# Pairs in the first feed-forward block, the norm's factor moved behind the products, and VectorE's pair work rearranged

## The chip, the cores and the metric

The kernel runs on one core of a Trainium2 chip. Its time is the device time of one execution in microseconds (us); before the change it is 1032.45 us, the median of 3 runs (1032.17 to 1032.88).

## What is computed

One trunk layer on x of shape (1, 256, 2048) in float32. A projection of the normed input feeds four differential-attention heads and a conformer convolution; their outputs, side by side, go through an output projection and are added to x, which gives h. Then comes the part that the change touches, a gated feed-forward block with 5632 hidden columns:

```
h  = h + mixed @ w_out
hn = rms_norm(h, norm2_g)              # h * rstd2 (per row) * g2 (per column)
a  = hn @ w_gate ;  bu = hn @ w_up     # 2048 -> 5632
y  = h + (silu(a) * bu) @ w_down
```

## The kernel before

**Precision by splitting.** Every operand of a matmul is split into a rounded part `hi` (float32r) and the remainder `lo`, and a product is three matmuls: hi*hi, lo*hi, hi*lo. ScalarE makes `whi` of the weights (L326), VectorE subtracts to get `wlo` (L335). For some units a second way makes `wlo`: ScalarE writes the negated weights (L329) and a DMA on GpSimd's queue adds the weights to it (L330); these are the units that `BY_DMA` names.

**Units.** The work is a list `chunks`, one entry per unit. A plain unit is two k-tiles (128 rows each) of one weight matrix times 512 columns: 2 x 2 x 3 = 12 matmuls of 128x512. `run_chunks` goes through the list with a hand-written order: at step t it splits units up to t + 2 and rounds units up to t + 2, or t + 3 when a pair is near (`lead`, `HI_AHEAD`, `LO_AHEAD`), then multiplies unit t. In the middle and at the end of a unit it calls `resume()`, which takes every running side generator one `yield` further; that is how sums, transposes and forms are put between units.

**Blocks.** The feed-forward part has 11 blocks j of 512 hidden columns, each with 16 gate and 16 up k-tiles, in three groups of 4, 4 and 3; after each group come two passes of the down projection. Blocks 1 to 10 and the down passes use a scheme of the Strassen kind: a *pair* takes k-tiles p and p + 8 of both matrices and makes 7 products (`PRODUCTS`, 21 matmuls) in place of 8 (24 matmuls). The other 8 k-tiles (`REST`, taken in twos) stay plain units, "g" for gate and "u" for up; "s" is a pair. `ORDER = "sggsggsuusuu"`, and block 1 has `FIRST_ORDER`. The products go to eight PSUM banks, `acc` for the first four and `aux` for the others; `bank_sums` (L1182) adds them on VectorE, `products_done` applies silu and `block_done` multiplies.

A pair costs VectorE and ScalarE this (`b` are the four loaded tiles, `t` four sums of them): three subtractions and additions (L1049 to L1051, `round_pair`), a cast of `b` on ScalarE (L1052), then in `split_pair` a cast of the sums (L1055) and the remainders `wlb` and `wlt` (L1058, L1059). `wt`, which holds `t`, has one buffer; `wb`, `wh`, `wlb` and `wlt` have two.

**Block 0** is plain: 8 gate units and 8 up units with `fh`, the split operands of h. The forms of h that pairs need, with the norm's factor `rstd2` multiplied in, are made beside it by `make_forms` (L984 to L1032): it spreads the factor over the columns by two transposes (L988), multiplies the rows by it (L996), and makes sums and splits. `out_done` runs after each of the four column groups n of the output projection: it adds to h (L828), transposes h (L846), scales by g2 (L851), splits (L853, L854), and copies h out to DRAM on GpSimd's queue (L823).

**Memory.** A pool `pre` holds everything up to the feed-forward part, h included; after the last column group it is closed and a pool `ffn` takes its place.

Of the kernel before, what the change touches and what calls it, by code (L numbers as in the profile page):

```python
# [18 lines left out]
P = 128  # L19
# [14 lines left out]
LINE = 128  # L34
EPS = 1e-6
# [51 lines left out]
FIRST_ORDER = "gsggsgsuusuu"  # L87
# [16 lines left out]
PAIR_BUFS = 2  # L104

# [24 lines left out]
def tile_block(  # L130
# [13 lines left out]
    prestack = ExitStack()  # L144
    pre = prestack.enter_context(tc.tile_pool(name="pre", bufs=2))
    small = prestack.enter_context(tc.tile_pool(name="small", bufs=4))
# [4 lines left out]
    h = [pre.tile([P, D], F32, tag=f"h{m}", name=f"h{m}", bufs=1) for m in range(NM)]  # L151
# [255 lines left out]
    def run_chunks():  # L407
# [4 lines left out]
        loaded, split = set(), set()  # L412
# [8 lines left out]
        def split_next():  # L421
            chunks[j]["split"](chunks[j])
            split.add(j)

# [3 lines left out]
        def freed(side, t):  # L428

            which, bufs = ((raws, RAW_BUFS), (pairs, PAIR_BUFS))[side]  # L430
            if not ahead[side] or pairs[2] - 1 not in loaded:
                return None
            k = which[place[side][ahead[side][0]] - bufs]
            return k if k in split and (t >= k or not chunks[k]["by_dma"]) else None

# [7 lines left out]
        for t in range(n):  # L443
# [33 lines left out]
    def square_sum(src, accum, **kw):  # L477
        junk = pre.tile([P, N], F32, tag="junk", name="junk", bufs=1)
# [107 lines left out]
    def conv_back(b):  # L586
# [37 lines left out]
        for b in range(2):  # L624
            for t in range(NB // 2):
# [6 lines left out]
                for j in range(2):  # L632
# [3 lines left out]
                    hi = pre.tile([P, S], F32R, tag="mchi", name=f"mchi{ct}", bufs=NCT)  # L636
                    lo = pre.tile([P, S], F32R, tag="mclo", name=f"mclo{ct}", bufs=NCT)
# [135 lines left out]
    def attend_values(hd):  # L773
# [29 lines left out]
        for e in range(2):  # L803
            mixa[2 * hd + e] = lhs_pair("a", 2 * hd + e) if hd >= 2 else tuple(
                pre.tile([P, S], F32R, tag=t, name=t, bufs=4) for t in ("mahi", "malo"))
# [7 lines left out]
    hT = {}  # L813

    hn = []
# [9 lines left out]
    def out_done(n, ps):  # L825
        cs = slice(n * N, (n + 1) * N)
# [13 lines left out]
        for t in range(0, N // P, 2):  # L840
# [6 lines left out]
            if k % HK == 0:  # L847
                hn.append(early.tile([P, HK, S], F32, tag="wb", name="hn"))
            rows = hn[k // HK][:, k % HK : k % HK + 2, :]
            for i in range(2):  # L850
                act.activation(rows[:, i, :], pt[:, i, :], AF.Copy, scale=col("g2", k + i))  # L851
            hi, lo = lhs_two("h", k)
            act.copy(hi, rows)  # L853
            dve.tensor_tensor(lo, rows, hi.bitcast(F32), ALU.subtract)  # L854
            for i in range(2):
                hT[k + i] = (hi[:, i, :], lo[:, i, :])
# [3 lines left out]
        else:  # L860
            yield
            yield
            prestack.close()
            ffn["pool"] = ctx.enter_context(tc.tile_pool(name="ffn", bufs=1))
            start(make_forms())


    ffn = {}
    actT = {}
    sil = {}  # L870

    def silu_done(ps):
        yield
        for m in range(NM):
            sil[m] = ffn["pool"].tile([P, N], F32, tag=f"sum{m}", name="sil")
            act.activation(sil[m], ps[m], AF.Silu, scale=rstd2[m])

    def up_done(j, ps):
        fp = ffn["pool"]
        aa = []  # L880
        for m in range(NM):
            a = fp.tile([P, N], F32, tag=f"sum{2 + m}", name="a")
            dve.scalar_tensor_tensor(a, ps[m], rstd2[m], sil[m], ALU.mult, ALU.mult)
            aa.append(a)
        yield from lag(4)
        yield from transposed(j, aa)

    def transposed(j, aa):
        last = j + 1 in FIRSTS and NDS[group_of(j)[0]] < HD
        b = j - group_of(j)[1]  # L890
        for t in range(N // P // 2):
# [9 lines left out]
            if b < 2 and 2 * t < nd:  # L901
                if not b and not t:
                    raw_act[g] = ffn["pool"].tile([P, 2, nd, S], F32, tag="draw", name="raw_act")
# [30 lines left out]
    def make_down_forms(g):  # L934
# [20 lines left out]
        hs = ffn["pool"].tile([P, 2, nd, P], F32R, tag="dhs", name="dhs")  # L955
# [12 lines left out]
        ls = ffn["pool"].tile([P, 4, nd, P], F32R, tag="draw", name="dls")  # L968
# [11 lines left out]
    def make_forms():  # L980
        fp = ffn["pool"]
        rep = fp.tile([P, S], F32, tag="sum1", name="rep")
        for m in range(NM):
            act.activation(rep[:, m * P : (m + 1) * P], ident, AF.Identity, bias=rstd2[m], scale=0.0)  # L984
        yield
        ps = aux_ps.tile([P, N], F32, tag="aux", name="ps_r")
        for m in range(NM):
            pe.transpose(ps[:, m * P : (m + 1) * P], rep[:, m * P : (m + 1) * P], ident)  # L988
        yield
        rb = fp.tile([P, S], F32, tag="sum2", name="rb")  # L990
        act.copy(rb, ps[:, :S])
        yield
        for i in range(2):
            for k in range(0, HK, 4):
                t = hn[i][:, k : k + 4, :]
                dve.tensor_tensor(t, t, rb.unsqueeze(1).to_broadcast([P, 4, S]), ALU.mult)  # L996
                yield

        nr = HK - NS
        chi = fp.tile([P, 2 * nr, S], F32R, tag="chi", name="chi")  # L1000
        clo = fp.tile([P, 2 * nr, S], F32R, tag="clo", name="clo")
        for i in range(2):
            act.copy(chi[:, i * nr : (i + 1) * nr], hn[i][:, NS:])
        yield
        for i in range(2):
# [370 lines left out]
```

## Time and profile before

| what | value |
|---|---|
| time, median of 3 | 1032.45 us |
| span of the profiled execution | 1030.8 us |
| TensorE (PE) busy | 1025.7 us, 100% |
| VectorE (DVE) busy | 929.2 us, 90% |
| ScalarE (ACT) busy | 643.4 us, 62% |
| GpSimd (POOL) busy | 102.7 us, 10% |
| block 0 begins / block 1 begins | 338.3 / 383.1 us |

Of the profiled execution the span from its first to its last instruction is known, and it lies 1.65 us under the median of the timed runs. In rows of the timeline the first number is the start in us, the second the duration, then engine, line, operation, output <- inputs, shape and count; brackets give the idle time before it and what ended it. Rows of the table by stage give, for each engine, busy us and in brackets the number of instructions.

### The profile page before, as it was taken

How to read it: one execution, taken by the hardware profiler on the slowest of the kernel's cores; microseconds unless marked ns; L12 is line 12 of the kernel's file. 1: busy time of each engine (PE TensorE's matmuls, PEld its weight loads, DVE VectorE, ACT ScalarE, POOL GpSimd, SP SyncE). 2: the span in 40 equal slices, each digit the busy share in tenths (PEclk: the TensorE clock that was granted, in tenths of full speed). 3: DMA queues.
4: the chain of work that ended last, by engine and by line, in shares of the span. 5: the costliest groups of instructions: out<-in, count | busy, mean ns of one | idle time of the engine just before them, and what ended most of it. 6: DMA issues, size and time to landing. Idle time of an engine off the chain costs nothing.

```text
span 1030.8 us, 13034 instructions
## 1 busy us (share of the span) xinstructions
PE 1025.7 (100%) x4642; PEld 849.4 (82%) x4642; DVE 929.2 (90%) x1128; ACT 643.4 (62%) x786; POOL 102.7 (10%) x146
## 2 busy tenths in 40 slices
PE   9999999999999999999999999999999999999998
PEld 8888888888888888888888888888888888888887
DVE  6899999999765699999999898989999989889998
ACT  7644656665756675676666556667757556657562
POOL 0300112111000000100102101101001111010020
PEclk9999999999999999999999999999999999999999
DMA  9757555544466677997989799889798979897776
GB/s 338 254 194 258 190 184 164 158 169 166 141 215 214 197 262 222 282 265 210 254 259 272 251 257 270 258 234 262 228 269 255 285 207 283 247 267 218 226 200 174
DMA packets 116448, 238.64 MB, mean 232 GB/s; under 512 B 7840, under 2 KB 9120, under 8 KB 116384
## 3 DMA queue, kind: packets, MB, share of 16 engines
q1 hardware_dynamic: 105216, 203.58, 59.3%
q0 software_dynamic: 10880, 34.08, 17.0%
q8 instruction: 36, 0.59, 0.2%
q14 instruction: 28, 0.23, 0.1%
q10 hardware_dynamic: 288, 0.16, 0.1%
HBM read 204.24 MB, written 9.44 MB: 207 GB/s over the span
## 4 chain that ended last, share of the span: by engine, by line
PE 100%; POOL 0%; DVE 0%; issue 0%; POOLq 0%
PE acc L365 11%; PE acc L366 11%; PE acc L371 11%; PE q L1097 11%; PE q L1103 11%; PE q L1098 11%; PE q L1078 9%; PE q L1077 9%; PE q L1076 9%; PE ps_a L898 1%; PE ps_s L712 1%; PE ps_o L782 1%; PE ps_warm L164 0%; PE ps_h L846 0%; PE ps_qk L693 0%; PE ps_at L802 0%
## 5 line engine op out<-in xcount | busy, mean ns | idle before, releaser
L326 ACT CAST whi<-raw 128x1024 fp32r<-128x1024 f32 (+1 forms) x256 | 264.2, 1043 | 143.8 <-PE acc L366 86.6
L335 DVE TENSOR_TENSOR wlo<-raw,whi 128x1024 fp32r<-128x1024 f32 (+1 forms) x208 | 250.4, 1214 | 38.2 <-ACT whi L326 38.0
L1055 ACT CAST wh<-wt 128x2048 fp32r<-128x2048 f32 x61 | 116.8, 1915 | 109.9 <-DVE wt L1051 109.7
L1059 DVE TENSOR_TENSOR wlt<-wt,wh 128x2048 fp32r<-128x2048 f32 x61 | 139.8, 2291 | 19.8 <-ACT wh L1055 19.7
L1097 PE MATMUL q<-whi,chi 128*128 128x512 f32 x320 | 125.2, 391 | 0.0
L1098 PE MATMUL q<-whi,clo 128*128 128x512 f32 x320 | 124.6, 389 | 0.0
L365 PE MATMUL acc<-whi,xhi 128*128 128x512 f32 x312 | 124.1, 398 | 0.0
L366 PE MATMUL acc<-whi,xlo 128*128 128x512 f32 x312 | 122.2, 392 | 0.0
L1076 PE MATMUL q<-wh,fhi 128*128 128x512 f32 x280 | 109.8, 392 | 0.0
L1077 PE MATMUL q<-wh,flo 128*128 128x512 f32 x280 | 109.0, 389 | 0.0
L1058 DVE TENSOR_TENSOR wlb<-wb,wh 128x1536 fp32r<-128x1536 f32 x61 | 106.8, 1751 | 1.0 <-ACT wh L1052 1.0
L572 DVE SCALAR_TENSOR_TENSOR y<-upad,cw,y 128x256 f32<-128x256 f32 x240 | 101.6, 490 | 0.0
L330 POOL DMA_DIRECT2D wlo<-raw x48 | 41.5, 865 | 555.7 <-ACT wlo L329 286.3
L1052 ACT CAST wh<-wb 128x1536 fp32r<-128x1536 f32 x61 | 89.8, 1472 | 1.0 <-DMA wb<-in_w_down_dram 1.0
L1103 PE MATMUL q<-wlo,chi 128*128 128x512 f32 x320 | 85.7, 390 | 0.0
L371 PE MATMUL acc<-wlo,xhi 128*128 128x512 f32 x312 | 85.2, 394 | 0.0
L1049 DVE TENSOR_TENSOR wt<-wb 128x1024 f32<-128x1024 f32 x61 | 74.4, 1220 | 0.0
L1097 PE MATMUL q<-whi,ahi 128*128 128x512 f32 x182 | 71.0, 390 | 0.0
L1098 PE MATMUL q<-whi,alo 128*128 128x512 f32 x182 | 70.9, 389 | 0.0
L1103 PEld LDWEIGHTS q<-wlo,chi 128*128 128x128 f32 x320 | 60.0, 188 | 12.7 <-DMA wlo<-raw 0.3
L1097 PEld LDWEIGHTS q<-whi,chi 128*128 128x128 f32 x320 | 60.1, 188 | 12.3
L1098 PEld LDWEIGHTS q<-whi,clo 128*128 128x128 f32 x320 | 60.1, 188 | 12.2
(260 smaller groups left out, 1850.5 us busy)
## 6 DMA issues: line engine op xcount, KB each, us to landing
raw<-in_w_in_dram SPq DMA_DIRECT2D x78, 512.0 KB, 4.6
raw<-in_w_gate_dram SPq DMA_DIRECT2D x48, 512.0 KB, 5.0
raw<-in_w_up_dram SPq DMA_DIRECT2D x48, 512.0 KB, 5.3
wlo<-raw POOLq DMA_DIRECT2D x48, 512.0 KB, 7.1
raw<-in_w_down_dram SPq DMA_DIRECT2D x46, 512.0 KB, 6.2
wb<-in_w_down_dram SPq DMA_DIRECT2D x42, 512.0 KB, 5.9
wb<-in_w_up_dram SPq DMA_DIRECT2D x40, 512.0 KB, 4.4
wb<-in_w_gate_dram SPq DMA_DIRECT2D x40, 512.0 KB, 5.5
```

The source lines that it names most:

```text
L326: act.copy(c["hi"], c["raw"])
L335: dve.tensor_tensor(c["lo"], c["raw"], c["hi"].bitcast(F32), ALU.subtract)
L365: pe.matmul(ps[m], xhi[:, ms], hi[:, j, :], start=c["first"] and j == 0, stop=False)
L366: pe.matmul(ps[m], xlo[:, ms], hi[:, j, :], start=False, stop=False)
L371: pe.matmul(ps[m], xhi[:, ms], lo[:, j, :], start=False, stop=c["last"] and j == nk - 1)
L1055: act.copy(c["hi"][:, :SUMMED], c["t"])
L1059: dve.tensor_tensor(lot, c["t"], c["hi"][:, :SUMMED].bitcast(F32), ALU.subtract)
L1076: pe.matmul(ps, hi, c["hi"][:, w], start=bool(first), stop=False)
L1077: pe.matmul(ps, lo, c["hi"][:, w], start=False, stop=False)
L1097: pe.matmul(ps, xs[i][0][:, ms], hi[:, i, :], start=i == 0 and bool(c["first"].get(qs[m])), stop=False)
L1098: pe.matmul(ps, xs[i][1][:, ms], hi[:, i, :], start=False, stop=False)
L1103: pe.matmul(sum_bank(c, qs[m]), xs[i][0][:, ms], lo[:, i, :], start=False, stop=i == 1 and bool(c["last"].get(qs[m])))
```

## The change

Block 0 becomes a block with pairs like the others, in the order `gugusgsgssuu`: four plain units first, on columns of h that the second column group provides. `make_forms` starts after the third column group and no longer needs the norm's factor: h's operands carry g2 alone, and the factor is applied as the scale of silu and once more by a copy on ScalarE, in every block. The two sets of PSUM banks change places in block 0. The first two pairs' weights are loaded five units ahead of block 0. Three of its plain units have their remainder made by DMA.

In every pair VectorE's work is cut finer and interleaved: the first subtraction stays in `round_pair`, the two further sums move to `split_pair` between pieces of the remainders, and the cast and the remainder of the first two sums come last (`finish_pair`), behind the next unit's cast on ScalarE. At a block's end `sums_aside` may let GpSimd make the sums of the next pair that is not yet begun, if its weights are loaded and the pair before it is finished. The order of two additions in `bank_sums` changes.

Pools: `pre` is closed at the first column group; h, the split mixed operands and small tiles go to a pool `keep` on the other side of the memory, whose place a pool `late` (sums, `wlb`, `wlt`, the down forms) takes after the last column group, waiting tile by tile.

```diff
+ORDERS = {0: "gugusgsgssuu", 1: "gsggsgsuusuu"}
+PAIRS_AHEAD = 5
 # run_chunks
+                if chunks[i].get("kind") == "s":
+                    finish()
                 chunks[i]["round"](chunks[i])
...
+            finish()
             load_freed(t)
+            if t == first - PAIRS_AHEAD:
+                for k in pairs[:PAIR_BUFS]:
+                    load(k)
 # out_done
+        if not n:
+            prestack.close()
+            ffn["pool"] = fp = ctx.enter_context(tc.tile_pool(name="ffn", bufs=1))
...
+            if k % HK < NS:
+                rows = ffn["rows"][:, k // HK, k % HK : k % HK + 2, :]
+                for i in range(2):
+                    act.activation(rows[:, i, :], pt[:, i, :], AF.Copy, scale=col("g2", k + i))
+            else:
+                a = REST.index(k)
+                hi, lo = (ffn[x][:, a : a + 2, :] for x in ("chi", "clo"))
+                for i in range(2):
+                    act.activation(hi[:, i, :], pt[:, i, :], AF.Copy, scale=col("g2", k + i))
+                for i in range(2):
+                    dve.scalar_tensor_tensor(lo[:, i, :], pt[:, i, :], col("g2", k + i), hi[:, i, :].bitcast(F32),
+                                             ALU.mult, ALU.subtract)
...
+        if n == HK * P // N:
+            yield
             start(make_forms())
+        if n == D // N - 1:
+            keepstack.close()
+            ffn["late"] = ctx.enter_context(tc.tile_pool(name="late", bufs=1, side="right", reuse_waits="tile"))
 # make_forms: rep, ps_r, rb, the products hn * rb, chi and clo are gone
 # round_pair
-        dve.tensor_tensor(t[:, 2:4], b[:, 1:3], b[:, 0:1].to_broadcast([P, 2, N]), ALU.subtract)
-        dve.tensor_tensor(t[:, 1], b[:, 1], t[:, 3], ALU.add)
-        dve.tensor_tensor(t[:, 0], t[:, 1], b[:, 3], ALU.subtract)
         act.copy(c["hi"][:, SUMMED:], b[:, 1:])
+        if "t" not in c:
+            first_sums(c, dve)
+    def first_sums(c, engine):
+        engine.tensor_tensor(t[:, 2:4], b[:, 1:3], b[:, 0:1].to_broadcast([P, 2, N]), ALU.subtract)
+    def last_sums(c, engine):
+        yield engine.tensor_tensor(t[:, 1], b[:, 1], t[:, 3], ALU.add)
+        yield engine.tensor_tensor(t[:, 0], t[:, 1], b[:, 3], ALU.subtract)
+    def sums_aside():
+        pairs = [c for c in chunks if c.get("kind") == "s"]
+        n = next((n for n, c in enumerate(pairs) if not c.get("rounded")), None)
+        if n and "b" in pairs[n] and "finished" in pairs[n - 1]:
+            c = pairs[n]
+            first_sums(c, pool)
+            c["summed"] = len(list(last_sums(c, pool)))
 # split_pair
+        sums = iter(()) if c.get("summed") else last_sums(c, dve)
+        act.copy(hi[:, 2:SUMMED], t[:, 2:])
+        rest(lob[:, :1], b[:, 1:2], hi[:, SUMMED : SUMMED + 1])
+        next(sums, None)
+        rest(lob[:, 1:], b[:, 2:], hi[:, SUMMED + 1 :])
+        next(sums, None)
+        rest(lot[:, 2:], t[:, 2:], hi[:, 2:SUMMED])
+    def finish_pair(c):
+        hi, t = c["hi"][:, :2], c["t"][:, :2]
+        act.copy(hi, t)
+        rest(c["lot"][:, :2], t, hi)
+        c["finished"] = True
 # sum_bank
-            tag, pool_ = ("acc", acc_ps) if i < 4 else ("aux", aux_ps)
+            tag, pool_ = ("acc", acc_ps) if (i < 4) != c["swap"] else ("aux", aux_ps)
 # bank_sums
+        dve.tensor_tensor(w1, q[Q2], w1, ALU.add)
         dve.tensor_tensor(w4, q[Q5], u3, ALU.add)
         dve.tensor_tensor(u2, q[Q5], u2, ALU.add)
-        dve.tensor_tensor(w1, q[Q2], w1, ALU.add)
         dve.tensor_tensor(u3, q[Q4], u3, ALU.add)
+        sums_aside()
 # products_done
-        for t in g:
-            act.activation(t, t, AF.Silu)
+        for m, t in enumerate(g):
+            act.activation(t, t, AF.Silu, scale=rstd2[m])
+            act.activation(t, t, AF.Copy, scale=rstd2[m])
 # the list of units
-            if j:
-                gate_up_block(j)
-                continue
-            block(w_gate, j * N, range(KD), fh, silu_done)
-            block(w_up, j * N, range(KD), fh, lambda ps, j=j: up_done(j, ps))
+            gate_up_block(j)    # block 0: by DMA g (12, 13), (14, 15) and u (12, 13); swap=True
```

More of the change, by code (lines that the diff above doesn't have):

```diff
@@ L34 @@
 LINE = 128
+EDGE = 320
 EPS = 1e-6
@@ L411, in run_chunks @@
         raws = [k for k in range(n) if chunks[k].get("kind") != "s" and not chunks[k].get("spare_raw")]
-        loaded, split = set(), set()
+        loaded, split, unfinished = set(), set(), []
+        first = min(k for k in range(n) if "kind" in chunks[k])
         def load(k):
@@ L846, in out_done @@
                     pe.transpose(pt[:, i, m * P : (m + 1) * P], h[m][:, (k + i) * P : (k + i + 1) * P], ident)
[L847 to L856, printed above, removed]
+            if k % HK < NS:
[10 more added lines that the diff above has]
+                                             ALU.mult, ALU.subtract)
+                    plain[k + i] = (hi[:, i, :], lo[:, i, :])
             yield
@@ L859, in out_done @@
             h_squares(n, cs)
-        else:
+        if n == HK * P // N:
             yield
-            yield
-            prestack.close()
-            ffn["pool"] = ctx.enter_context(tc.tile_pool(name="ffn", bufs=1))
             start(make_forms())
+        if n == D // N - 1:
+            keepstack.close()
+            ffn["late"] = ctx.enter_context(tc.tile_pool(name="late", bufs=1, side="right", reuse_waits="tile"))
     ffn = {}
+    plain = {}
     actT = {}
[L870 to L886, printed above, removed]
     def transposed(j, aa):
@@ L981, in make_forms @@
         fp = ffn["pool"]
[L982 to L1005, printed above, removed]
-            dve.tensor_tensor(clo[:, i * nr : (i + 1) * nr], hn[i][:, NS:],
-                              chi[:, i * nr : (i + 1) * nr].bitcast(F32), ALU.subtract)
-            yield
-        forms.update(plain={k: (chi[:, i, :], clo[:, i, :]) for i, k in enumerate(REST)})
-        a11, a21 = (hn[0][:, :NS, m * P : (m + 1) * P] for m in range(NM))
-        a12, a22 = (hn[1][:, :NS, m * P : (m + 1) * P] for m in range(NM))
+        rows = ffn["rows"]
+        a11, a21 = (rows[:, 0, :, m * P : (m + 1) * P] for m in range(NM))
+        a12, a22 = (rows[:, 1, :, m * P : (m + 1) * P] for m in range(NM))
         fhi = fp.tile([P, 7, NS, P], F32R, tag="fhi", name="fhi")
@@ L1062, in sum_bank, with rest @@
+    def finish_pair(c):
[3 more added lines that the diff above has]
+        c["finished"] = True
+    def rest(lo, raw, h):
+        dve.tensor_tensor(lo, raw, h.bitcast(F32), ALU.subtract)
     def sum_bank(c, i):
@@ L1069, in multiply_pair @@
     def multiply_pair(c):
-        while (fs := c["pairs"]()) is None:
+        while (fs := c["pairs"]()) is None or len(plain) < len(REST):
             resume()
@@ L1131, in multiply_two, with fast_block @@
             start(c["done"](c["sums"]))
-    def fast_block(order, pairs, twos, sources, operands, half, whole, by_dma=dict(g=(), u=())):
+    def fast_block(order, pairs, twos, sources, operands, half, whole, by_dma=dict(g=(), u=()), swap=False):
         units, sums = [], {}
@@ L1138, in fast_block @@
             what = left[kind].pop(0)
-            c = dict(kind=kind, sums=sums, done=None, first={}, last={}, rows=what["rows"], **operands)
+            c = dict(kind=kind, sums=sums, swap=swap, done=None, first={}, last={}, rows=what["rows"], **operands)
             if kind == "s":
@@ L1158, in gate_up_block @@
     def gate_up_block(j):
-        fast_block(ORDER if j > 1 else FIRST_ORDER, [dict(p=p, rows=slice(p, p + HK + 1, HK)) for p in range(NS)],
+        fast_block(ORDERS.get(j, ORDER), [dict(p=p, rows=slice(p, p + HK + 1, HK)) for p in range(NS)],
                    [dict(ks=ks, rows=slice(ks[0], ks[1] + 1, ks[1] - ks[0]), k=ks) for ks in TWOS],
                    dict(g=(w_gate, j * N), u=(w_up, j * N)),
-                   dict(pairs=lambda: forms.get("pair"), plain=lambda k: forms["plain"][k]),
+                   dict(pairs=lambda: forms.get("pair"), plain=plain.get),
                    products_done, lambda sums: block_done(j, sums),
-                   BY_DMA if j > 1 and j not in FIRSTS else dict(g=(), u=BY_DMA["u"]))
+                   BY_DMA if j > 1 and j not in FIRSTS else dict(g=(), u=BY_DMA["u"]) if j else
+                   dict(g=TWOS[2:], u=TWOS[2:3]), swap=not j)
     def down_pass(g, j0, nb):
@@ L1183, in bank_sums @@
     def bank_sums(q):
-        w1, u2, u3, w4 = (ffn["pool"].tile([P, N], F32, tag=f"sum{i}", name=f"sum{i}") for i in range(4))
+        w1, u2, u3, w4 = (ffn["late"].tile([P, N], F32, tag=f"sum{i}", name=f"sum{i}") for i in range(4))
         act.copy(w1, q[Q1])
```

55 lines of the change are left out of this document (33 added, 22 removed).

## The prediction

> **What bounds the kernel now.** I read the page's busy times first, then its chain, then a table by stage, then single rows of the timeline around block 0.
>
> ```profile
> PE 1025.7 (100%) x4642; PEld 849.4 (82%) x4642; DVE 929.2 (90%) x1128; ACT 643.4 (62%) x786; POOL 102.7 (10%) x146
> PE 100%; POOL 0%; DVE 0%; issue 0%; POOLq 0%
> core 0: us, PE busy (x) PEld busy (x) DVE busy (x) ACT busy (x) POOL busy (x), PEclk, DMA share, GB/s
> 338.30:382.50 44.20, 44.20 (x201) 36.47 (x200) 36.86 (x40) 29.05 (x39) 1.99 (x4) 1.00 0.69 221
> 424.85:466.60 41.75, 41.75 (x190) 34.58 (x188) 39.05 (x39) 29.56 (x30) 3.42 (x4) 1.00 0.91 263
> 466.60:508.30 41.70, 41.70 (x189) 34.57 (x188) 40.17 (x41) 27.95 (x27) 3.35 (x4) 1.00 0.80 231
> ```
>
> TensorE is busy for 1025.7 of 1030.8 us and the chain that ends last is TensorE alone, at a granted clock of 1.00. So time can only be won by giving TensorE fewer instructions, and is lost wherever another engine makes it wait. The table is read by VectorE's column: 36.9 of 44.2 us in nearly all of the old block 0, but 39.1 of 41.8 and 40.2 of 41.7 in blocks that already use pairs. A block with pairs has VectorE 94 to 96% full. The change makes block 0 such a block.
>
> The profiled span is 1030.8 us and the median of the timed runs 1032.45; I keep the 1.65 between them as a constant.
>
> **What TensorE loses (a sure gain).** Block 0 was 16 plain units (8 gate, 8 up) of 12 matmuls; it becomes 8 plain units and 4 pairs of 21. That is 192 against 96 + 84 = 180 matmuls.
>
> ```profile
> 334.68 1.07 PE L371 MATMUL acc<-wlo,mchi 128*128 128x512 f32 x4
> 337.40 1.07 PE L371 MATMUL acc<-wlo,mchi 128*128 128x512 f32 x4
> ...
> 346.58 1.07 PE L371 MATMUL acc<-wlo,hhi 128*128 128x512 f32 x4
> 349.30 1.07 PE L371 MATMUL acc<-wlo,hhi 128*128 128x512 f32 x4
> 352.28 1.07 PE L371 MATMUL acc<-wlo,hhi 128*128 128x512 f32 x4
> ```
>
> Second halves of successive plain units start 2.72 us apart, so a matmul costs 2.72 / 12 = 0.227 us: 12 fewer save 2.72. Between 349.30 and 352.28 lie 2.98 us, because the two transposes that spread the norm's factor (L988) stand there; they go too: 0.26. Together 2.98 us. No step adds TensorE work.
>
> **What hides VectorE's other edits.** Durations by size:
>
> ```profile
> 378.23 1.22 DVE L1049 TENSOR_TENSOR wt<-wb 128x1024 f32<-128x1024 f32 x1
> 379.48 0.69 DVE L1050 TENSOR_TENSOR wt<-wb,wt 128x512 f32<-128x512 f32 x1
> 380.21 0.69 DVE L1051 TENSOR_TENSOR wt<-wt,wb 128x512 f32<-128x512 f32 x1
> 381.95 1.75 DVE L1058 TENSOR_TENSOR wlb<-wb,wh 128x1536 fp32r<-128x1536 f32 x1
> 383.62 2.29 DVE L1059 TENSOR_TENSOR wlt<-wt,wh 128x2048 fp32r<-128x2048 f32 x1
> 123.33 0.42 DVE L682 TENSOR_TENSOR t<-acc,gcsk 128x256 f32<-128x256 f32 x1
> ```
>
> A pair's VectorE work was 1.22 + 0.69 + 0.69 + 1.75 + 2.29 = 6.64 us; cut finer it is 4 x 1.22 + 3 x 0.69 = 6.95. But L1050 starts 1.25 after L1049 and L1051 0.73 after that, each behind the result it reads, while independent neighbours overlap by about 0.1; with the pieces interleaved those gaps go, so I take the cost per pair as zero, between -0.2 and +0.3. ScalarE's cast of the sums, cut in two and put behind the next unit's cast, delays nothing of TensorE's: the first product needs the sums' remainder, which VectorE finished last before as well. The two scalings by the factor that each block gains on ScalarE run while VectorE adds; ScalarE is 62% busy. Casts to plain operands straight from PSUM, and the multiplication by the factor that goes, take load off VectorE (the four multiplications of L996 have L1049's size).
>
> **Block 0's first pair (a loss).** It stands behind four plain units, so it starts four units after the last output-projection matmul, and VectorE's queue decides whether it is ready. That queue can be read off the old trace:
>
> ```profile
> 338.69 1.23 DVE L335 TENSOR_TENSOR wlo<-raw,whi 128x1024 fp32r<-128x1024 f32 x1 [1.49 <-ACT whi L326]
> 339.83 1.28 DVE L828 TENSOR_TENSOR h<-h,acc 128x512 f32<-128x512 f32 x2
> 343.43 0.69 DVE L854 TENSOR_TENSOR hlo<-hn,hhi 128x512 fp32r<-128x512 f32 x1 [1.22 <-ACT hhi L853]
> ...
> 341.93 0.82 ACT L851 ACTIVATE hn<-ps_h,cols 128x256 f32<-128x256 f32 x2
> ...
> 341.03 0.67 PE L846 MATMUL ps_h<-ident,h 128*128 128x128 f32 x4
> 343.40 0.60 PE L846 MATMUL ps_h<-ident,h 128*128 128x128 f32 x4
> ```
>
> TensorE begins block 0 at 337.40 + 0.91 = 338.31. The additions to h end at 341.1, the transposes follow at 341.0 to 341.5, ScalarE scales them from 341.93; VectorE's first remainder from PSUM (0.42, L682's size) can start at 342.4, the second ends near 343.2. Then, in program order: the first pair's subtraction (to 344.4), unit 3's remainder (345.5), two more remainders of 0.42, which wait for the second transposes and for ScalarE, itself behind two long casts (about 346.4), and the pair's six pieces, 0.69 + 0.69 + 1.22 + 0.69 + 1.22 + 1.22 less 0.5 of overlap: about 351.6. TensorE reaches the pair at 338.31 + 4 x 2.72 + 2 x 0.44 for the transposes + 0.2 = 350.3 and needs the sums' remainder with its third matmul, at 350.7. So it waits 0.9; I take 0.8, from 0 (if VectorE gets ahead in the projection's last units) to 1.5.
>
> The pieces also land in memory that h held. The last copies of h go out through GpSimd's queue:
>
> ```profile
> 340.80 1.14 POOL L823 DMA_DIRECT2D hd<-h  x2 [21.66 <-DVE h L828]
> DMA to landing us min/median/max: 3.9/5.0/6.8
> ```
>
> Two issues to 341.9, landing 3.9 to 6.8 later: 345 to 348.7. The pair's first piece starts near 346.4, so this costs 0, at worst 2.3.
>
> **The rest of block 0, and block 1.** Making the forms (eight of 0.69 and one of 1.75, 7.3 us of VectorE) now falls in the projection's last units, where VectorE idles 1.5 us per unit (the row at 338.69); it pushes the addition to h some 0.3 later, and with it the transposes and, by the exchanged banks, the second unit's first matmul. I price this at 0.3, from 0 to 0.5. Pairs two and three have 10.2 us of TensorE each time a plain unit lies between and about 8 of VectorE; the fourth follows the third directly and arrives with none to spare. Block 0's end now has six additions from PSUM more:
>
> ```profile
> 461.13 0.69 DVE L1188 TENSOR_TENSOR sum<-q,sum 128x512 f32<-128x512 f32 x1
> 464.53 0.68 DVE L1193 TENSOR_TENSOR sum<-q,sum 128x512 f32<-128x512 f32 x1
> 386.28 0.39 PE L1078 MATMUL q<-wlt,fhi 128*128 128x512 f32 x1
> 477.72 0.39 PE L1078 MATMUL q<-wlt,fhi 128*128 128x512 f32 x1
> 474.43 2.29 DVE L1059 TENSOR_TENSOR wlt<-wt,wh 128x2048 fp32r<-128x2048 f32 x1 [0.73 <-ACT wh L1055]
> ```
>
> They take 461.13 to 465.2, 4.1 us. Block 1's first pair had its remainder at 383.62 + 2.29 = 385.91, 0.37 before its use at 386.28, and pays those additions from the idle time that VectorE gains by having 3 of 8 plain remainders done by DMA. I put 0.2 on all of this, 0 to 1.
>
> Loads move too. The first two pairs' four loads of 512 KB are issued five units before block 0, on SP's queue in front of those of three plain units.
>
> ```profile
> raw<-in_w_gate_dram SPq DMA_DIRECT2D x48, 512.0 KB, 5.0
> ```
>
> At 263 GB/s for a DMA share of 0.91 the engines move some 289 GB/s (an estimate from the table), so these 2.1 MB take 7.3 us. A plain load is issued when one of five buffers comes free, some five units (13.6 us) ahead, and lands in 5.0: 8.6 to spare, so 0. The three DMA remainders of block 0 start three units ahead, over 8 us before use, and land in 7.1 (row below): 0 as well, up to 2 at the longest landing.
>
> **The sums on GpSimd.** At each block's end where the next block opens with a pair, three sums of its second pair (2.60 us) leave VectorE; I count 14 such places, none of them at the end of block 0. This pair is the tightest of a steady block: 474.43 + 2.29 = 476.72 against 477.72, 1.0 to spare, so TensorE wins nothing by it. No such sum on GpSimd is in the trace; the nearest rows:
>
> ```profile
> 36.82 0.32 POOL L201 TENSOR_TENSOR gcsq<-rt,gb 128x64 f32<-128x64 f32 x1
> 37.10 1.30 POOL L202 TENSOR_TENSOR gcsq<-rt,gb 128x64 f32<-128x64 f32 x1
> 38.37 0.46 POOL L200 TENSOR_TENSOR gcsq<-rt,gb 128x128 f32<-128x128 f32 x1
> ...
> 36.90 1.32 DVE L335 TENSOR_TENSOR wlo<-raw,whi 128x1024 fp32r<-128x1024 f32 x1 [1.71 <-ACT whi L326]
> 38.15 0.86 DVE L550 SCALAR_TENSOR_TENSOR u<-acc,rstd,sig 128x256 f32<-128x256 f32 x2
> ...
> 465.58 0.86 POOL L330 DMA_DIRECT2D wlo<-raw  x1 [3.58 <-ACT wlo L329]
> DMA to landing us min/median/max: 5.6/7.1/10.3
> 476.36 1.07 PE L1103 MATMUL q<-wlo,chi 128*128 128x512 f32 x4
> ```
>
> 64 elements more cost 0.14 us, 2.1 ns each, so 1024 take 0.46 + 896 x 0.0021 = 2.4 and 512 take 1.3: 5.0 in all, from 461.1 (when the previous pair's sums are read) to 466.1. Behind them on GpSimd's queue stands the DMA remainder of the second gate unit: issued at 465.58 so far, then at 466.2, landed by 473.3 (7.1), needed at 476.36. That holds, so I cost it at 0.
>
> The row at 37.10 warns: 64 elements took 1.30 instead of 0.32, ending 0.18 after VectorE's two-SBUF-input instruction of 36.90 to 38.22, while 38.37 ran at full speed beside L550, which reads PSUM. So such VectorE instructions keep GpSimd out, and the additions from PSUM, 461.1 to 465.2, let it in; just there the sums are issued. The Trainium skill ("GPSIMD Engine Reference", section 1, Specifications) has this as a rule, that the SBUF interfaces are shared and contended with VectorE instructions of two SBUF inputs; this trace agrees at 37.10, and by the rule alone VectorE at 95% would starve the sums, which is the last rival below.
>
> **Sum.** 1030.8 - 2.98 + 0.8 (first pair) + 0.3 (addition to h) + 0.2 (tight pairs) = 1029.1 of span, + 1.65 = 1030.8. Anything nearer than about 0.2% (2.1 us) this kernel's measurement hardly tells from no change.
>
> **Rivals.** (1) The main case, 1030.4 to 1031.6: the first pair is late and takes a good third of the gain. Chance 0.40. (2) VectorE gets ahead, and nothing waits: 1032.45 - 2.98 = 1029.5, or up to 1030.4 with half the losses. For it: VectorE's idle 1.5 us a unit before block 0. Against: it waits there for TensorE to free buffers, and cannot run far ahead. Chance 0.34. (3) h's copies land at 6.8 or the tight pairs all miss: 2.3 + 0.8 + 1 eat the gain, 1032.5, no change. Chance 0.09. (4) Slower: GpSimd's two small sums don't get in before 465.2 and must wait until VectorE's products from SBUF are through:
>
> ```profile
> 467.55 1.29 DVE L1214 TENSOR_TENSOR sum<-sum,sum 128x512 f32<-128x512 f32 x2
> ```
>
> From 468.8 they take 2 x 1.3, the DMA behind them issues at 471.4 and lands at 478.5, 2.1 after its use at 476.36; in 14 places 30 us: 1060. It decides from an issue later than 469.2; halfway (470) it costs 0.7 x 14 = 10, 1041. For it: 37.10. Against: the additions from PSUM stand right beside the sums. Chance 0.17.
>
> **Numbers.** Main case 1030.8. Faster by over 0.2% (under 1030.4): rival 2 and the main case's edge, 0.38. Within: 0.45. Slower: rival 4, 0.17. The main case's own range is 1030.2 to 1031.8; for 8 in 10 it runs from 1029.2 (nothing waits, 0.3 lower for the small waits that the old block 0 had) over the no-change case to the first part of rival 4, 1036.
>
> **What would show it.** TensorE has some 14 instructions fewer, no L988. Right: a gap of 0.5 to 1 us before the third matmul of block 0's first pair, released by VectorE's last piece; block 1's pairs tight; GpSimd's sums 5 us long, ended before the products at a block's end. Wrong for rival 2: no gap there. Wrong for rival 4: TensorE's remainder matmuls of the second gate unit wait for a DMA in each block.

## The result, and the profile after

The changed kernel takes 1041.27 us (median of 4 runs, 1040.95 to 1041.48), the kernel before 1032.43 beside it: ratio 1.0085, 95% interval 1.007 to 1.010. The forecast was 1030.8 us, in a range that ended at 1036.0. The profiled execution's span is 1039.2 us, 8.4 more than before. First its busy times and its chain:

```profile
PE 1026.9 (99%) x4628; PEld 847.0 (82%) x4628; DVE 908.9 (87%) x1227; ACT 670.7 (65%) x864; POOL 178.8 (17%) x191
PE 93%; DVE 3%; DMA 2%; ACT 1%; issue 0%; SPq 0%; DVEq 0%; ACTq 0%
```

TensorE has 4628 instructions, 14 fewer, as it should, yet the chain that ends last is no longer TensorE alone: VectorE, DMA and ScalarE hold 6% of it. Who TensorE waited for (in all, times, longest, in us):

```profile
PE q L1093 <- ACT wh L1072: 3.3, 2, 2.9
PE q L1095 <- DVE wlt L1077: 1.1, 2, 0.5
PE q L1114 <- DVE sum L1211: 1.0, 1, 1.0
PE q L1114 <- DVE sum L1208: 0.5, 1, 0.5
PE ps_h L867 <- DVE h L849: 0.3, 1, 0.3
```

These waits are few. Set against the old trace, the starts of the same transposes (L906, before L898) show where the time went: after block 0 TensorE is 0.36 us ahead (388.19 against 388.55), near 935 it is 0.48 ahead (935.11 against 935.59). So the ten blocks behind block 0 neither win nor lose more than 0.1 us, and all of the loss, some 8.9 us, lies in the last 80 us: a first part near 963, a second near 1015, and 0.9 us at the very end, where the last copy of the output lands 2.8 us after its issue instead of 2.0.

**Near 963 us.** VectorE's rows ahead of the last block's sums of banks, before:

```profile
953.44 0.55 DVE L964 SCALAR_TENSOR_TENSOR dlo<-raw_act,dhi 128x384 fp32r<-128x384 f32 x1
953.91 0.55 DVE L966 TENSOR_TENSOR dlo<-dsums,dhi 128x384 fp32r<-128x384 f32 x1
...
957.96 0.69 DVE L1188 TENSOR_TENSOR sum<-q,sum 128x512 f32<-128x512 f32 x1 [0.95 <-ACT sum L1186]
```

and after, with GpSimd's rows and the two of TensorE that waited:

```profile
953.55 3.20 DVE L972 SCALAR_TENSOR_TENSOR dlo<-raw_act,dhi 128x384 fp32r<-128x384 f32 x1
953.60 2.73 POOL L1038 TENSOR_TENSOR wt<-wb 128x1024 f32<-128x1024 f32 x1
956.41 1.50 POOL L1042 TENSOR_TENSOR wt<-wb,wt 128x512 f32<-128x512 f32 x1
956.68 1.65 DVE L974 TENSOR_TENSOR dlo<-dsums,dhi 128x384 fp32r<-128x384 f32 x1
957.99 1.49 POOL L1043 TENSOR_TENSOR wt<-wt,wb 128x512 f32<-128x512 f32 x1
...
961.89 0.68 DVE L1206 TENSOR_TENSOR sum<-q,sum 128x512 f32<-128x512 f32 x1
...
964.11 0.47 PE L1114 MATMUL q<-whi,ahi 128*128 128x512 f32 x1 [0.50 <-DVE sum L1208]
965.81 0.50 PE L1114 MATMUL q<-whi,ahi 128*128 128x512 f32 x1 [1.00 <-DVE sum L1211]
```

VectorE's instruction of two SBUF inputs took 3.20 us instead of 0.55: it ends at 956.75, behind GpSimd's first sum (953.60 + 2.73 = 956.33). At the other 13 places GpSimd's first sum had to wait for VectorE's last remainder (`POOL wt L1038 <- DVE wlt L1077: 46.0, 13, 16.0` in the list of waits), and so ran beside the additions from PSUM; here it had nothing to wait for and began beside VectorE's work from SBUF. VectorE's next instructions are stretched too, the sums of banks begin 3.9 us later, and TensorE, which wants their banks for the first plain units of the down projection, loses 1.8 us in two steps of 0.88 and 1.40 where 0.23 is usual.

**Near 1015 us.** In these rows `hd` is the copy of h in DRAM, to which DMAs on GpSimd's queue add finished sums (`hd<-sum`, the accumulations), and `hend` is the part of it that is loaded back at the end. The last pair's weights, before (timeline, then the landing times of the two loads):

```profile
994.17 1.75 DVE L1058 TENSOR_TENSOR wlb<-wb,wh 128x1536 fp32r<-128x1536 f32 x1
995.70 2.13 POOL L1242 DMA_DIRECT2D hd<-sum  x2
996.00 0.93 SPq L1039 DMA_DIRECT2D wb<-in_w_down_dram  x2
1005.85 1.48 ACT L1052 CAST wh<-wb 128x1536 fp32r<-128x1536 f32 x1 [1.05 <-DMA wb<-in_w_down_dram]
```

```profile
DMA to landing us min/median/max: 6.9/8.1/9.3
```

and after, in the same two views:

```profile
997.28 2.10 POOL L1262 DMA_DIRECT2D hd<-sum  x2
997.89 0.69 DVE L1043 TENSOR_TENSOR wt<-wt,wb 128x512 f32<-128x512 f32 x1
998.65 1.66 SPq L1020 DMA_DIRECT2D wb<-in_w_down_dram  x2
1013.13 1.49 ACT L1031 CAST wh<-wb 128x1536 fp32r<-128x1536 f32 x1 [5.85 <-DMA wb<-in_w_down_dram]
1017.00 0.69 DVE L1043 TENSOR_TENSOR wt<-wt,wb 128x512 f32<-128x512 f32 x1
1017.73 1.04 ACT L1072 CAST wh<-wt 128x1024 fp32r<-128x1024 f32 x1 [1.21 <-DVE wt L1043]
1018.82 0.50 PE L1093 MATMUL q<-wh,dhs 128*128 128x512 f32 x1 [2.90 <-ACT wh L1072]
1020.08 0.74 PE L1095 MATMUL q<-wlt,dhs 128*128 128x512 f32 x1 [0.53 <-DVE wlt L1077]
```

```profile
DMA to landing us min/median/max: 9.0/11.5/13.9
```

The load is issued at 998.65 instead of 996.00, and takes 13.9 us to land instead of 9.3. The delay near 963 moved the accumulations by 1.58 us (997.28 instead of 995.70); against the first of them the load comes 1.07 us later, 1.37 behind it instead of 0.30. Its buffer is last read by L1043, the second of the two sums that moved to `split_pair` (997.89 to 998.58); before, that was the remainder `wlb`, ended at 995.92. TensorE waits 2.90 us for ScalarE's cast of the sums and then 0.53 for their remainder. Behind the wait it also runs slowly; in the table by stage the columns are the stretch, its length, busy us and instructions of PE, PEld, DVE, ACT and POOL, then the granted clock, the DMA share and GB/s:

```profile
1010.00:1015.00 5.00, 5.00 (x24) 4.13 (x23) 1.57 (x2) 1.86 (x2) 0.58 (x1) 1.00 1.02 308
1015.00:1019.00 4.00, 1.10 (x6) 0.60 (x5) 4.00 (x6) 2.79 (x4) 0.54 (x1) 1.00 0.89 253
1019.00:1024.00 5.00, 4.47 (x12) 3.23 (x13) 4.43 (x4) 1.76 (x2) 0.00 (x0) 0.66 0.28 80
```

The granted clock is 0.66 from 1019 to 1024: seven steps from one matmul to the next of 0.427 us instead of 0.227, 1.4 us more.

### The profile page after: what moved, and what is told of

The parts are those of the page before. It is cut to its first block, busy times and chain, and to the rows that moved or that the text cites. A ratio compares the mean times of both kernels' runs of the same rounds, so it can differ in the third digit from the quotient of the medians.

```text
span 1039.2 us, 13227 instructions
## 1 busy us (share of the span) xinstructions
PE 1026.9 (99%) x4628; PEld 847.0 (82%) x4628; DVE 908.9 (87%) x1227; ACT 670.7 (65%) x864; POOL 178.8 (17%) x191
## 4 chain that ended last, share of the span: by engine, by line
PE 93%; DVE 3%; DMA 2%; ACT 1%; issue 0%; SPq 0%; DVEq 0%; ACTq 0%
PE q L1120 11%; PE q L1114 11%; PE q L1115 11%; PE q L1095 10%; PE q L1093 10%; PE q L1094 10%; PE acc L369 9%; PE acc L370 9%; PE acc L375 9%; DMA wb<-in_w_down_dram 1%; PE ps_a L906 1%; DMA raw<-in_w_in_dram 1%; PE ps_s L730 1%; PE ps_o L800 0%; DVE wlt L1077 0%
## 5 line engine op out<-in xcount | busy, mean ns | idle before, releaser
L330 ACT CAST whi<-raw 128x1024 fp32r<-128x1024 f32 (+1 forms) x248 | 258.2, 1044 | 165.9 <-PE acc L370 69.5
L339 DVE TENSOR_TENSOR wlo<-raw,whi 128x1024 fp32r<-128x1024 f32 (+1 forms) x197 | 236.8, 1212 | 39.1 <-ACT whi L330 34.8
L1077 DVE TENSOR_TENSOR wlt<-wt,wh 128x1024 fp32r<-128x1024 f32 x130 | 157.6, 1222 | 20.1 <-ACT wh L1061 14.4
L1077 DVE TENSOR_TENSOR wlb<-wb,wh 128x512 fp32r<-128x512 f32 (+1 forms) x130 | 122.8, 953 | 26.4 <-ACT wh L1031 26.3
L1114 PE MATMUL q<-whi,chi 128*128 128x512 f32 x352 | 137.8, 391 | 0.0
L1115 PE MATMUL q<-whi,clo 128*128 128x512 f32 x352 | 137.0, 389 | 0.0
L1093 PE MATMUL q<-wh,fhi 128*128 128x512 f32 x308 | 120.8, 392 | 0.4 <-ACT wh L1072 0.4
L1094 PE MATMUL q<-wh,flo 128*128 128x512 f32 x308 | 119.9, 389 | 0.0
L1072 ACT CAST wh<-wt 128x1024 fp32r<-128x1024 f32 x65 | 68.4, 1052 | 47.3 <-DVE wt L1043 46.3
L1120 PE MATMUL q<-wlo,chi 128*128 128x512 f32 x352 | 94.5, 390 | 0.0
L1061 ACT CAST wh<-wt 128x1024 fp32r<-128x1024 f32 x65 | 68.3, 1051 | 23.9 <-DVE wt L1038 23.9
```

Of the source, the lines that this page charges most:

```text
L330: act.copy(c["hi"], c["raw"])
L339: dve.tensor_tensor(c["lo"], c["raw"], c["hi"].bitcast(F32), ALU.subtract)
L1077: dve.tensor_tensor(lo, raw, h.bitcast(F32), ALU.subtract)
L1093: pe.matmul(ps, hi, c["hi"][:, w], start=bool(first), stop=False)
L1094: pe.matmul(ps, lo, c["hi"][:, w], start=False, stop=False)
L1114: pe.matmul(ps, xs[i][0][:, ms], hi[:, i, :], start=i == 0 and bool(c["first"].get(qs[m])), stop=False)
```

## The experiments

Theory A: two separate losses, GpSimd's sums at one place, and the late load. A1, its closer form: the load is dear because it falls behind the two accumulations `hd<-sum` on GpSimd's queue. Rivals are named in the expectations.

**1 to 4: each suspected part undone alone, and both.** Without GpSimd's sums anywhere, and without them in the last block only:

```diff
 # bank_sums (run 1; in run 2 only where j + 1 == sum(FGROUPS))
-        sums_aside()
```

> The changed kernel without any pair sums on GpSimd (all on VectorE). Theory A (two losses: at 953 us GpSimd's sums lengthen VectorE's instructions, which costs TensorE 2 us near 963; near 1015 the last pair's weights are loaded late, because the sums moved into split_pair keep their buffer; 6 us with what follows): the stall near 963 goes, the one near 1015 stays, 1041.3 - 2 = 1039.3 us. Rival B (GpSimd's sums are the whole loss, the late load follows from the stall near 963): 1032. Rival C (they pay in the steady blocks, through VectorE's time): over 1041.3, with new waits for wlt in the blocks.

> The changed kernel with GpSimd's sums kept in all blocks but the last gate/up block (one place, 953 us). Theory A: like the run without any GpSimd sums, 1039.3 us: the other 13 places neither cost nor win. Rival B: 1032. Rival C: below the run without any by 0.3 us or more.

Measured: 1038.51 (ratio 1.0058, 1.0043 to 1.0073) and 1038.54 (1.0057, 1.0042 to 1.0072). 2.7 us come back in both, and the wait near 963 is gone; the one near 1015 stays (3.3 and 3.4 us). So one place of 14 costs it all. Then the two sums back in their old place, in the last group's passes:

```diff
 # round_pair
             first_sums(c, dve)
+            if c.get("inline"):        # pairs of the last group's down passes
+                c["summed"] = len(list(last_sums(c, dve)))
```

> The changed kernel, but in the three-block group's down passes the pair's two last sums stand on VectorE directly behind the first ones, as before, not between the remainders. Theory A: the last pair's load is issued 1 us earlier and lands before its use; the wait of 3.1 + 0.7 us near 1015, the slow clock behind it (1.6) and the longer tail (0.9) go, the 2 us near 963 stay: 1035 us. Rival D (the load is late because it meets the DMAs to and from hd, whatever the order of the sums): it is only 1.1 us earlier, 1039 to 1040. Rival B: no change, 1041.

> Both edits: no GpSimd sums in the last gate/up block, and the two last sums first in the last group's passes. Theory A: both losses go, and what block 0 won stays: 1032.0 us, 0.4 below the kernel before. Rival D: 1036 or more, with a wait for the last pair's weights left. Rival B: like the run with the first edit alone.

Measured: 1034.93 (1.0026, 1.0016 to 1.0036) and, with both edits, 1031.89 (0.9996, 0.9986 to 1.0005). Undone alone, the sums' place is worth 6.3 us and GpSimd's sums 2.7; both together give 9.4. Of the 2.7, the steps near 963 are some 2 us and the last copy of the output 0.9: it lands in 1.9 us in runs 1, 2 and 4 and in 2.9 in run 3. That GpSimd's sums lengthen this copy is not shown, for in run 8, which has none at 953, it took 2.8 too. In the third run, in these two views again:

```profile
997.31 2.10 POOL L1264 DMA_DIRECT2D hd<-sum  x2
997.48 0.89 SPq L1020 DMA_DIRECT2D wb<-in_w_down_dram  x2
1007.35 1.49 ACT L1031 CAST wh<-wb 128x1536 fp32r<-128x1536 f32 x1 [2.36 <-PE q L1117]
```

```profile
DMA to landing us min/median/max: 7.2/8.2/9.3
```

An issue 1.17 us earlier is a landing 5.8 us earlier (997.9 + 9.3 against 999.1 + 13.9): the load now goes out 0.17 us behind the first accumulation instead of 1.37. With both edits the waits near 963 and 1015 are gone, and the time is that of the kernel before within what can be told.

**5 and 6: what makes the load slow.** The accumulations put behind the load, or hend's loads taken out of its neighbourhood:

```diff
 # down_half (run 5)
-            yield from lag(HD_LAG)
+            yield from lag(HD_LAG + 3 * (g == len(FGROUPS) - 1))
 # run 6: fetch_end() is called at the end of the last block_done, not in down_whole
```

> The changed kernel with one thing moved: the first two hd<-sum accumulations of the last group's first pass stand on GpSimd's queue behind the second two, so that the last pair's weights are issued before any of them; the order of the pair's sums stays. So far a load issued 0.2 us behind the first accumulation took 9.3 to 10.1 us to land, one issued 1.4 us behind it 13.9 to 14.4. Theory A1 (the place in the DMA queues against the accumulations decides, the sums' order only moves the load past them): it lands within 10 us of its issue, before 1009, the wait near 1015 goes to under 0.7 us, the clock stays at 1.00: 1035 us, like the run with the sums first. Theory A2 (the load's own lateness of 1 to 2.6 us and the loads of hend behind it decide): 1039 to 1041.

> The changed kernel with the four loads of hend (1 MB) issued at the end of the last gate/up block, some 25 us earlier, so that they don't stand behind the last pair's weights. Theory A2 (hend's loads share the DMA engines with the weights): the weights land 3 to 4 us earlier and the wait near 1015 goes: 1035 to 1036 us. Theory A1 (the accumulations to hd do it): the weights still land over 12 us after issue, 1040 to 1041.

Measured: 1035.82 (1.0031, 1.0019 to 1.0044) and 1041.46 (1.0086, 1.0072 to 1.0100). Run 5, with the sums as late as in the changed kernel, in the two views:

```profile
998.66 1.62 SPq L1020 DMA_DIRECT2D wb<-in_w_down_dram  x2
1001.90 1.77 POOL L1290 DMA_DIRECT2D hd<-sum  x2 [4.30 <-DVE sum L1278]
1003.10 2.35 POOL L1262 DMA_DIRECT2D hd<-sum  x2
1007.20 1.47 ACT L1031 CAST wh<-wb 128x1536 fp32r<-128x1536 f32 x1
```

```profile
DMA to landing us min/median/max: 5.9/6.8/7.7
```

The same issue time as after, and it lands in 7.7 us. In run 6 it took 14.5, with a wait of 3.5. So A1 holds: with the same order of the sums and the same time of issue, the place against the accumulations alone made the load fast. hend's loads have no part.

**7 and 9: parts of the change put into the kernel before.**

```diff
 # run 7: round_pair -> start of split_pair
+        dve.tensor_tensor(t[:, 1], b[:, 1], t[:, 3], ALU.add)
+        dve.tensor_tensor(t[:, 0], t[:, 1], b[:, 3], ALU.subtract)
         act.copy(c["hi"][:, :SUMMED], c["t"])
 # run 9: split_pair and finish_pair as in the change, sums on VectorE; block 0 as before
```

> The kernel before with one part of the change alone: the pair's two last sums moved from round_pair to the start of split_pair, everywhere; nothing cut finer, block 0 untouched, nothing on GpSimd. Theory A: the steady blocks don't notice (VectorE does the same work in another order), but in the last pass the weights' buffer comes free 1.3 us later, the load falls behind the accumulations, and TensorE waits near 1014 for 3 to 4 us and loses 1 to 2 to the clock: 1037 to 1038 us. Rival E (the late load is due to other parts of the change, such as the casts in two pieces): 1032.4 to 1033.

> The kernel before with the change's handling of a pair alone (sums between the remainders, casts of the sums behind the next unit's), all on VectorE; block 0 plain as before, nothing on GpSimd. Theory A1: the steady blocks take the same time, and the last pair's weights are issued 1.2 us or more later than in the kernel before, behind both accumulations to hd, and land over 13 us after issue; TensorE waits 3 to 4 us near 1015 and runs slowly behind it: 1038.5 to 1039.5 us, the run without GpSimd sums (1038.5) plus block 0's small gain. Rival F (block 0's change, by moving everything earlier against the DMAs, has a part in the late load): 1033 or less.

Measured: 1040.2 (1.0071, 1.0057 to 1.0084) and 1038.88 (1.0061, 1.0047 to 1.0075). Run 7 came out slower by another way than I wrote (timeline, GpSimd and TensorE):

```profile
1001.19 0.88 POOL L330 DMA_DIRECT2D wlo<-raw  x1 [11.14 <-ACT wlo L329]
1011.09 1.30 PE L1104 MATMUL q<-wlo,ahi 128*128 128x512 f32 x4 [3.32 <-DMA wlo<-raw]
```

Its load was ahead of the accumulations and landed in 7.1 us. But ScalarE's cast of all four sums now waited 5.47 us for VectorE at the head of its queue, and the negated copy behind it, and with it the DMA remainder of a plain unit, came 6 us late (995.15 before). The change avoids this one by casting the late sums in `finish_pair`. Run 9 is the clean test: the new pair handling alone, on the old block 0, costs 6.3 us, with the load 1.57 us behind the first accumulation, 13.8 us to land and a wait of 2.8 us. Block 0 has no part in the late load.

The load's time against its place, from all traces:

| load issued, against the first hd<-sum | kernels | second load lands after |
|---|---|---|
| 3.0 to 3.2 us ahead | runs 5, 7 | 7.1 to 7.7 us |
| 0.2 to 0.3 us behind | before, runs 3, 4, 8, 10, 11, 12, 14, 15 | 8.9 to 10.1 us |
| 1.4 to 1.6 us behind | after, runs 1, 2, 6, 9, 13 | 13.8 to 14.5 us |

The landings (time of issue plus time to landing) show what the first load's place changes. Issued 0.2 to 0.3 us behind the first accumulation, it is ahead of the second, and in the kernel before both loads land, at 1002.9 and 1005.7, ahead of both accumulations, at 1006.7 and 1008.7. Issued 1.4 us behind the first, it is behind both, and in the changed kernel each load lands behind an accumulation: accumulation 1005.8, load 1007.6, accumulation 1011.0, load 1013.0. Every run has the order of its row of the table.

**8 and 10 to 15: block 0's gain.** All but run 13 start from the run with both edits at the end, or from run 11, which has no sums on GpSimd at all.

> No GpSimd sums anywhere, and the two last sums first in the last group's passes: against the run with both edits at the end this takes GpSimd's sums from the other 13 places too. Theory A: they neither cost nor win, 1031.9 us within 0.3. Rival C (they relieve VectorE in the blocks): 1032.5 or more. Rival: they cost in small waits, 1031.3 or less.

Run 11: 1032.42 (0.9998, 0.9989 to 1.0006): the other 13 places neither cost nor win that can be told. One more plain unit ahead of the first pair (order `guguusgsgssu`):

> The run with both edits at the end, and block 0's order guguusgsgssu, the first pair behind five plain units instead of four. Theory: the waits at the first pair (0.56 + 0.70 us over a matmul's 0.23, near 351) go, 1.3 us; from 0 to 1.0 of it comes back at block 1's first pair, which now has one plain unit less behind block 0's last pair: 1030.9, from 1030.6 to 1031.9 us. Rival: block 1's pairs become late by more than was won, 1032 to 1033.

Measured: 1034.74 (1.0021, 1.0012 to 1.0030), a miss. The waits at the first pair went, and came back as others: 0.7 for a DMA remainder, 0.7 and 0.6 for the sums of banks at block 1's start; and the last copy of the output took 0.9 us longer. One more remainder by DMA (g=TWOS[1:]):

> The run with both edits at the end, and in block 0 the second gate unit's remainder too made by DMA instead of VectorE (ScalarE writes it negated, GpSimd issues the accumulation). Theory: VectorE reaches the addition to h 1.1 us earlier, which takes away the wait of 0.3 us at the transposes and 1.1 of the 1.3 us at the first pair: 1030.5 to 1030.9 us. Rival: the DMA is issued behind the copies of h on GpSimd's queue, or ScalarE's extra 1.05 us delays the scaling of h: the waits stay or a new one for wlo appears, 1031.9 or more.

Measured: 1032.20 (0.9997, 0.9988 to 1.0006): the rival. VectorE came to h some 1 us earlier, the first pair no longer waited, and TensorE waited 0.9 for that DMA and 0.5 at the fourth pair instead. Then the order of the products:

```diff
+SUMS_LAST = tuple(PRODUCTS[n] for n in (6, 4, 5, 1, 2, 0, 3))
 # multiply_pair
+        late = (Q1 not in c["first"] or c["swap"]) and (Q1 not in c["last"] or c.get("final"))
-        for n, (q, f, w) in enumerate(PRODUCTS):
+        for n, (q, f, w) in enumerate(SUMS_LAST if late else PRODUCTS):
```

> The run with no GpSimd sums and the last group's sums first, and the pair's seven products in another order: those of the plain rows of the weights first, those of the two last sums at the end; in all pairs but a block's first one (block 0's first has it too) and its last one (the last pass's last has it too). Theory G (block 0 lost its gain because the first product needs the operand that is ready last): the waits at block 0's first pair (0.56 + 0.70) and most of the 0.25 at the second go, TensorE needs the two last sums' operands 3.4 us later: 1032.4 - 1.5 = 1030.9 us. Rival H (VectorE is late with everything there, so the wait moves to the products behind, or to block 1): 1032 or more.

> The changed kernel with nothing else than that order of the products. Theory A1: the last pair's weights still land about 13 us after their issue, near 1012, but the pair's first product needs only the plain row's remainder, some 2.5 us after landing, and the last sums' operands 3.4 us later than now: the wait near 1015 falls from 3.8 to under 1 us and the clock stays at 1.00; the 2 us near 963 stay: 1041.3 - 1.5 (block 0) - 5 = 1034.5 to 1036 us. Rival H: the pair waits as long for other operands, 1039 or more.

Measured: 1032.55 (1.0005, 0.9996 to 1.0014; the profiled execution, 1035.3, is its slowest) and 1037.61 (1.0050, 1.0035 to 1.0066). In run 13 the load still took 14.2 us, but the pair waited 0.5 us and the clock stayed at 1.00: 3.7 us came back, block 0's first pair included, where at least 5.3 had been forecast. Run 12 came out at rival H's time. Its profiled execution is 2.8 us slower than its median, so it shows what can be late in block 0, not what the usual execution loses. The first pair no longer waits there, and the next thing that is late shows, in the list of TensorE's waits and in the table by stage:

```profile
PE q L1124 <- DMA wlo<-raw: 2.6, 2, 2.1
```

```profile
368.00:372.00 4.00, 4.00 (x12) 3.15 (x11) 4.00 (x5) 4.00 (x6) 0.85 (x1) 0.59 0.80 245
```

Block 0's fourth gate unit waits 2.1 us for its DMA remainder, and the granted clock was 0.59 behind it. Two runs put a remainder back on VectorE:

> The run with the products' other order, and block 0's third gate unit (the plain unit between its first and second pair) with its remainder on VectorE instead of by DMA. There the DMA, issued at 357.1 and 9.4 us under way, was waited for by 2.1 us. Theory G (the first pair's wait is set by the order, and the DMA remainder is merely the next thing that is late): that wait goes, VectorE has the 1.1 us because the pairs' last operands are now needed 3.4 us later: 1032.5 - 1.5 = 1031.0 us, from 1030.7 to 1031.5. Rival H (VectorE has no time left in block 0): the wait moves to the second or third pair, 1032 or more.

> As the run before it, but with the fourth gate unit's remainder on VectorE and the third's by DMA again: the DMA issued at 357.1 that was waited for is the fourth unit's (between the second and third pair), the run before took the wrong one. Theory G: the wait near 365 goes, VectorE has the 1.1 us: 1031.0 us, from 1030.7 to 1031.5. Rival H: VectorE has no time left and the wait moves to the third or fourth pair or to block 1, 1032 or more.

Measured: 1033.43 (1.0011, 1.0002 to 1.0020) and 1034.17 (1.0016, 1.0007 to 1.0025). Run 14 took the wrong unit and still waited 1.8 us for the fourth's DMA; run 15 took the right one, in its profiled execution (1033.16, below the median) that wait went, and the fourth pair was late instead (list of TensorE's waits):

```profile
PE q L1097 <- ACT wh L1075: 1.3, 1, 1.3
PE q L1099 <- DVE wlt L1080: 0.5, 1, 0.5
```

Both runs came out as rival H. In the profiled executions of runs 8, 10, 12 and 15 the wait that an edit removed came back as another, for a DMA remainder, at a later pair or at block 1's start, which fits VectorE and the DMA being both near their limit in block 0. No version beat the kernel before by more than can be told.

## Why the prediction was wrong, point by point

- **TensorE's 14 instructions** were right, and so was that nothing in it was added.
- **The first pair** was seen, and too small: 0.8 us forecast, 1.26 measured (0.56 + 0.70). The timeline of the changed kernel:

```profile
343.28 0.88 DVE L878 SCALAR_TENSOR_TENSOR clo<-ps_h,cols,chi 128x256 fp32r<-128x256 f32 x2 [0.57 <-ACT chi L876]
350.07 2.42 DVE L1077 TENSOR_TENSOR wlt<-wt,wh 128x1024 fp32r<-128x1024 f32 x2
350.19 1.05 ACT L1072 CAST wh<-wt 128x1024 fp32r<-128x1024 f32 x1 [1.05 <-DVE wt L1043]
351.29 0.50 PE L1093 MATMUL q<-wh,fhi 128*128 128x512 f32 x1 [0.40 <-ACT wh L1072]
352.55 0.50 PE L1095 MATMUL q<-wlt,fhi 128*128 128x512 f32 x1 [0.53 <-DVE wlt L1077]
366.45 1.19 PE L1120 MATMUL q<-wlo,chi 128*128 128x512 f32 x4
378.94 1.21 PE L1120 MATMUL q<-wlo,chi 128*128 128x512 f32 x4
```

VectorE's pieces ended at 352.5, not 351.6, and the 0.9 us were lost ahead of them: the first remainder from PSUM, forecast at 342.4, began at 343.28, because the addition to h came 0.5 later and VectorE waited until both of ScalarE's scalings were through (342.43 to 343.25), not the first alone. And that ScalarE's cut and moved cast of the sums "delays nothing of TensorE's" was wrong here: the first product waited for L1072, which follows the last sum, before it waited for the remainder.
- **The addition to h**: 0.3 forecast; it began at 340.33 instead of 339.83, and TensorE lost some 0.5 (the second L867 starts 0.60 us after the first, at 341.66, where 0.11 is usual).
- **Tight pairs**: 0.2 forecast, nothing measured: pairs two to four and block 1's first pair show no wait. The sum behind it was wrong as well: from one pair's start to the next, with a plain unit between, TensorE has 21 + 12 matmuls, 7.5 us and not 10.2. Rival 3's sum is off too: 2.3 + 0.8 + 1 is 4.1, 1.1 more than the gain, which makes 1033.6 and not 1032.5.
- **The DMA remainders**, priced at zero, cost some 0.5. They landed 9.4 and 8.6 us after their issue and not 7.1, at 366.40 and 378.90, and the matmuls of 366.45 (fourth gate unit) and 378.94 (third up unit) stood behind them: 0.25 and 0.23 us over the usual steps. Run 12 shows the first of the two as the next bound. (The expectation of run 12 places these 0.25 us at the second pair; the rows place them here.) With smaller steps of some 0.1 us block 0 lost 2.6 us more than the old one to waits, and 0.36 of the 2.98 was left; the forecast left 1.68.
- **The failed step: "with the pieces interleaved those gaps go, so I take the cost per pair as zero".** I priced VectorE's durations and TensorE's first product, not the buffer: moving the two sums past the sums of banks makes them the last reader of `wb`, and `wb` coming free is what issues the next load. In the steady blocks that costs nothing (0.36 us ahead at 388, 0.48 at 935); in the last pass, where the load meets the accumulations, it cost 6.3 us (runs 3 and 9). The prediction read no row of the last 80 us. The rows were there: the last load issued at 996.00, 0.3 behind an accumulation, with its cast waiting 1.05 us for it.
- **GpSimd's sums at zero** was right in 13 places and wrong in one. Their usual length was right (5.0 us forecast); the groups of GpSimd's rows of each line, with min, median and max in ns:

```profile
L1038 POOL TENSOR_TENSOR wt<-wb x14: 2406/2413/2743, 419.8 to 953.6; 128x1024 f32<-128x1024 f32 x14
L1042 POOL TENSOR_TENSOR wt<-wb,wt x14: 1295/1304/1498, 422.3 to 956.4; 128x512 f32<-128x512 f32 x14
L1043 POOL TENSOR_TENSOR wt<-wt,wb x14: 1288/1300/2169, 423.7 to 958.0; 128x512 f32<-128x512 f32 x14
```

That is 2.41 + 2 x 1.30 = 5.0. Rival 4 had the right resource and the wrong victim: it feared that VectorE keeps GpSimd out and a DMA behind GpSimd is late. VectorE did hold GpSimd up at some places, its last sum to 2.17 us where a VectorE subtraction of two SBUF inputs ran beside it, but no matmul of a steady block waited for a DMA by it. At 953 the two begin within 0.05 us of each other, and VectorE's instruction ends only behind GpSimd's; taking these sums away won 2.7 us of the time (run 2). That the measured 1041 equals rival 4's price halfway is chance, for the wait that it names stood nowhere. The Trainium skill ("SBUF — State Buffer", section "SBUF: two separate sides") says that whichever of the two starts first holds the shared ports for its whole instruction; the rows of 953 agree that the loser waits for a whole one, 3.20 us against 2.73, and don't tell who was first: by the recorded starts VectorE was, by 0.05 us. GpSimd's own sum took 2.73 instead of 2.41, so it was not free of delay either.
- **Loads, copies of h** at zero: in block 0 no wait for either is in the trace.

## What to carry to other kernels

When work is moved within one engine's order, ask which buffer it is now the last to read, and which load waits for that buffer; then look at the place where that load has least time, here the end of the kernel, where no later work could take up the delay. Before giving work to GpSimd beside a full VectorE, look at every place where it will run: beside additions that read PSUM it cost nothing, and at the one place where it began beside an instruction with two operands from SBUF it held VectorE up until its own sum was through. Where two engines and the DMA are all near their limit, a removed wait can return one step later, so price the block by its fullest engine and not by TensorE's instructions.

## What the runs showed of the hardware

- Two loads of 512 KB, the first issued 1.4 us behind the first of two accumulating DMAs and so behind both: the second of them landed 13.8 to 14.5 us after its issue. With the first issued 0.2 us behind that accumulation and ahead of the other one, it was 8.9 to 10.1 (table above). The Trainium skill ("DMA: Bandwidth & Descriptors", section on queues, rings and completion order) says that the DMA engines take turns between queues packet by packet; that alone doesn't tell why 1.2 us at the issue became 5 at the landing, and no run here does: why is open.
- TensorE's clock fell behind waits of 2.1 us (run 12) and 2.9 us (after): seven steps of about 0.427 us each time. So it did behind the waits of 2.8 to 3.5 us in runs 1, 2, 6, 7 and 9. Behind waits of 1.0 to 1.8 us (963 in the changed kernel, runs 14 and 15) the steps stayed at 0.227. The Trainium skill ("TensorE: Matmul & The Clock Gate", Part 1) puts the drop at an idle window of some 3.4 us; here less was enough.
